# A two-layer diffusion trunk on one core: VectorE's head factors and scalings moved to other places, the convolution's tap split over two engines, a state-space product in two halves, and a shorter inverse root

## The chip, the cores and the metric

The kernel runs on one core of a Trainium2 chip. The metric is the device time of one execution in microseconds, as a median of several runs. A core has five engines that run their own instruction queues in order and meet at semaphores: TensorE (PE, its weight loads PEld), VectorE (DVE), ScalarE (ACT), GpSimd (POOL) and SyncE (SP), which here issues all DMAs.

## The reference, cut to what matters

Two layers. Each normalises and modulates the stream (512 latent and 256 context tokens, width 1024), projects it, runs four mixers on the projection, merges them by gates, and ends with a SwiGLU network. The change touches the inverse roots of all norms and these parts of three mixers:

```python
def rms_norm(x, g, eps=1e-6):
    y = xf * lax.rsqrt(jnp.mean(xf * xf, axis=-1, keepdims=True) + eps)
    return (y * g.astype(jnp.float32)).astype(x.dtype)

def sgu_branch(z, lp):                      # spatial gating
    u, v = jnp.split(jax.nn.gelu(z), 2, axis=-1)
    v = layer_norm(v, lp['sgu_ln_g'], lp['sgu_ln_b'])
    ...

def prep(p):                                # state-space duality
    z, xbc, dt_raw = split_cols(p, (BR_W, SSD_CONV_CH, 2 * SSD_HEADS))
    xbc = jax.nn.silu(conv_centred(xbc, lp['ssd_conv_w'], lp['ssd_conv_b']))   # three taps along the tokens
    ...
    return (y_diag + y_off).reshape(b, L, H, P), final      # ssd_scan: within a block, and from the state before it

def mla_qkv(p, lp):                         # latent attention, 6 heads
    q = (rms_norm(cq, lp['mla_q_a_norm']) @ lp['mla_w_uq']).reshape(bsz, L, MLA_HEADS, MLA_QK)
    kv = (rms_norm(ckv, lp['mla_kv_a_norm']) @ lp['mla_w_ukv']).reshape(bsz, L, MLA_HEADS, MLA_NOPE + MLA_V)
    k_nope, v = jnp.split(kv, [MLA_NOPE], axis=-1)
    k = jnp.concatenate([k_nope, jnp.broadcast_to(k_rope[:, :, None, :], ...)], axis=-1)
    return rms_norm(q, lp['mla_q_norm']), rms_norm(k, lp['mla_k_norm']), v

def rope_2d(t, cos, sin):                   # latent tokens only
    nope, rot = t[..., :MLA_NOPE], t[..., MLA_NOPE:]
    x1, x2 = jnp.split(rot, 2, axis=-1)
    return jnp.concatenate([nope, x1 * c - x2 * s, x1 * s + x2 * c], axis=-1)

def softmax_attend(q, k, v):
    pr = jax.nn.softmax(s, axis=-1).astype(v.dtype)
    return jnp.einsum('bhqk,bkhd->bqhd', pr, v)
```

## The kernel before, in words

All large products are made of three: weights and streams are split into a high and a low part (`whi`, `wlo`; `h`), and `mm3` adds low times high, high times high and high times low into one bank of PSUM. `proj` does this for one tile of 128 columns, 512 latent tokens and then 256 context tokens, in a bank named `acc`, of which there are two; smaller work takes one of four banks `b`, and the diagonal state space two more. A callback then takes the result out of the bank; the next product that wants the bank waits for the last read of it.

A layer's mixing (`mix`) is a set of generators that one loop advances in turn: the projections, latent attention's first half (`mla`: queries, then keys and values, two token tiles at a time in `mla_pair`), the diagonal state space (`five`), attention itself (`attend`, one unit for two heads and 256 queries in `attend_unit`, six to nine units a layer), spatial gating (`sgu`), the projections with the convolution (`conv`), and the dual state space (`ssd`). The order in which the instructions stand on each engine is made when the program is built, by a list scheduler with a time model of its own, from priorities that follow the code and `at(...)`. On the chip each engine then keeps that order.

The places that the change touches:
- `rsqrt`: a bit trick on the vector engine and three Newton steps of three operations, with `-x/2` made once: 11 instructions. It stands in 44 places, on tiles of 1 to 12 columns: 7 in `norm_mod`, 10 in `ssd`, 5 in `sgu`, and two for each of the 11 pairs of `mla_pair` (six in layer 0, five in layer 1).
- `mla_pair`, second half: `rr`, an inverse root for each token and head, goes over q or k together with the gain `gn` (`qn`, `kn`: the 96 gains, the same for all heads, on all partitions), by one `s.stt` for each head and tile: 12 a pair. The rotary key is multiplied by its gains into `kg`. GpSimd rotates with cosines and sines from the constant tile `k`. Six transposes bring a tile to [96, head, token]; ACT takes three of the heads out of PSUM, DVE the other three.
- `mla_pair`, first half: `v` goes out of PSUM with the factor `r`, by DVE: `s.ts(vt[:, b, hs, :], pv[:, :, 64:P], r[:, b:b + 1])`.
- `attend_unit`: ACT makes the exponentials with their sums, DVE adds the two sums and takes the reciprocal, and DVE multiplies each tile of probabilities (128 x 768, or 128 x 256 for context) by it, in place: four a unit. Their transposes come one unit later.
- `sgu`: DVE subtracts the mean and multiplies by the inverse root.
- `conv`: five operations on the result of a projection, in `cb`: DVE makes the middle tap with the bias out of `acc`, adds the left and the right tap, ACT writes the tanh back into `acc`, and DVE makes `(tanh + 1) a` from it.
- `ssd`: for every block of 128 tokens and each of three column tiles, a product with the identity brings `yoff` into the bank, and four products of 64 columns add the rest.

Of the kernel before, what the change touches and what calls it, by code (L numbers as in the profile page):

```python
# [19 lines left out]
P = 128  # L20
# [47 lines left out]
def pieces(segs):  # L68
    """starts of the 256-token pieces"""
    return [t for off, n, _ in segs for t in range(off, off + n, 256)]  # L70


class Cut:
    """one row of tokens in several tiles: [(first token, count, tile)]"""
# [11 lines left out]
class Net:  # L86
# [117 lines left out]
    def rsqrt(s, y, x):  # L204
        shape = list(x.shape)
        hx, t = s.ty(shape), s.ty(shape)
        s.ts(y.bitcast(I32), x.bitcast(I32), -0.5, float(0x5F3759DF), ALU.mult, ALU.add)
        s.ts(hx, x, -0.5)
        for _ in range(3):
            s.mul(t, y, y)  # L210
            s.mul(t, t, hx)
            s.stt(y, t, 1.5, y, ALU.add, ALU.mult)
# [54 lines left out]
    def tok_rsqrt(s, sq, nb, mul, eps):  # L267
        """per token (token-major) rsqrt(mul * sum over partitions and given tiles + eps)"""
# [50 lines left out]
    def params_rest(s, l, loaded):  # L319
# [19 lines left out]
        q["qn"], q["kn"] = bc("qn", t["mla_q_norm"][l], 96), bc("kn", t["mla_k_norm"][l], 96)  # L339
# [43 lines left out]
    def ada_chunk(s, a, i, raw=None):  # L383
        """columns 256 i .. of the modulation"""
# [26 lines left out]
    def cuts(s, segs, count):  # L411
        """rows of tokens in f tiles"""
# [35 lines left out]
    def norm_mod(s, xs, gs, sh, segs, hh, hl):  # L448
        """hi and lo of the modulated norm, a segment a step"""
# [23 lines left out]
    def weights(s, ap, c0, width, kt=KD, step=P, e=()):  # L473
        """yields (hi, lo, m) of the column tiles of ap[:, c0:c0+width]"""
# [35 lines left out]
    def gelu2(s, out, x):  # L510
        """2 gelu(x)"""
# [5 lines left out]
    def sgu_prep(s, l, q):  # L517
        """the spatial weights transposed; the bias takes in the layer norm's offset"""
# [17 lines left out]
    def sgu(s, q, wsT, uvd, segs, yd):  # L536
        for t0 in pieces(segs):
# [14 lines left out]
            s.rsqrt(r, x)  # L552
            for j in range(2):
                s.ts(vn[:, j, :], vn[:, j, :], mv[:, j, 0:1], r[:, j:j + 1], ALU.subtract, ALU.mult)
# [14 lines left out]
    def mla(s, l, q, xd, kd, segs, qk):  # L569
        """xd: cq^T and ckv^T in DRAM; kd: token-major [P, NB, 44] with the rotary key"""  # L570
# [27 lines left out]
    def mla_pair(s, part, q, kd, off, t0, b0, xd, nk, nw, wh, wl, qk):  # L598
        """two token tiles from t0: q or k, v, normalised, rotated, transposed"""
# [19 lines left out]
        for b in range(2):  # L619
# [3 lines left out]
            for j in range(2):  # L623
# [7 lines left out]
                if part == "kv":  # L631
                    s.ts(vt[:, b, hs, :], pv[:, :, 64:P], r[:, b:b + 1])
# [16 lines left out]
        gn = q["qn"] if part == "q" else q["kn"]  # L649
        e = s.nc.gpsimd  # L650
        for b in range(2):
            x, full = tiles[b]
            tb = t0 + b
            for h in range(6):
                s.stt(x[:, h, :w], x[:, h, :w], rr[:, b, h:h + 1], gn[:, :w], ALU.mult, ALU.mult)
            if part == "kv":
                kg = s.ty([P, 1, 32])
                s.mul(kg, kr[:, b:b + 1, :], gn[:, 64:].unsqueeze(1))
                s.mul(x[:, :, 64:96], kg.to_broadcast([P, 6, 32]), rs[:, b, :].unsqueeze(2).to_broadcast([P, 6, 32]))
            if off == CTX:  # L660
                cs, sn = (s.k[:, j + 16 * (b0 + b):j + 16 * (b0 + b) + 16].unsqueeze(1).unsqueeze(1).to_broadcast([P, 6, 2, 16])
                          for j in (K_COS, K_SIN))
# [10 lines left out]
            s.act(y[:, 0:3], ps[0][:96])  # L673
            s.vcopy(y[:, 3:6], ps[1][:96])
# [23 lines left out]
    def attend_unit(s, c, t0, nk, qs, ks, vs, yd):  # L698
        """two heads, 256 queries"""
        scale = 96.0 ** -0.5  # L700
        pr = []
        for h2 in range(2):
# [23 lines left out]
            for b in range(2):  # L726
                s.ts(p[b][:, :nk * P], p[b][:, :nk * P], ri[:, b:b + 1])
# [17 lines left out]
    def ssd(s, l, q, zd, xd, cd, kd, segs, yd):  # L745
        """zd: 2 silu(z)^T, xd: x^T and B^T, cd: C^T by group (zero rows of the other), all in DRAM; kd: token-major dt"""
# [828 lines left out]
```

## Time and profile before

| | |
|---|---|
| median of 3 runs | 2835.06 us (2834.6 to 2836.26) |
| the profiled execution: span from first to last instruction | 2833.9 us, 1.2 us under the median |
| TensorE matmul busy | 2639.4 us (93%) |
| VectorE busy | 1562.5 us (55%) |
| ScalarE, GpSimd busy | 870.4 us (31%), 1210.8 us (43%) |
| mean granted TensorE clock | 0.974 of full speed |

A busy time is the union of an engine's rows. A matmul's row covers its way through the array, so neighbouring rows overlap and a busy TensorE is not one at its peak. Behind a row stands the idle time of its engine just before it, and what ended it. The granted clock is 1 at 2.4 GHz and 0.5 at 1.2 GHz.

### The profile page before, as it was taken

How to read it: one execution, taken by the hardware profiler on the slowest of the kernel's cores; microseconds unless marked ns; L12 is line 12 of the kernel's file. 1: busy time of each engine (PE TensorE's matmuls, PEld its weight loads, DVE VectorE, ACT ScalarE, POOL GpSimd, SP SyncE). 2: the span in 40 equal slices, each digit the busy share in tenths (PEclk: the TensorE clock that was granted, in tenths of full speed). 3: DMA queues.
4: the chain of work that ended last, by engine and by line, in shares of the span. 5: the costliest groups of instructions: out<-in, count | busy, mean ns of one | idle time of the engine just before them, and what ended most of it. 6: DMA issues, size and time to landing. Idle time of an engine off the chain costs nothing. (4 is left out here: it accounts for less than half of the span.)

```text
span 2833.9 us, 40144 instructions
## 1 busy us (share of the span) xinstructions
PE 2639.4 (93%) x14950; PEld 2147.7 (76%) x14950; DVE 1562.5 (55%) x3402; ACT 870.4 (31%) x1693; POOL 1210.8 (43%) x901
## 2 busy tenths in 40 slices
PE   6998898999999987999999999899999989899999
PEld 4777676777888875888888877777666866678887
DVE  6678989758453769543221245677836546422111
ACT  4233332342232333222212234333343223322222
POOL 2254444314432836554333334442423537344543
PEclk9999899999999998999999999999999989999999
DMA  7655454454444645323322335556445536323332
GB/s 247 175 176 188 138 168 141 145 162 143 138 155 149 213 139 169 108 91 94 97 76 60 94 98 159 179 175 192 139 152 167 167 127 206 114 84 105 104 97 82
DMA packets 430106, 397.46 MB, mean 140 GB/s; under 512 B 52292, under 2 KB 379640, under 8 KB 429816
## 3 DMA queue, kind: packets, MB, share of 16 engines
q1 hardware_dynamic: 429912, 394.91, 45.4%
q8 instruction: 118, 1.93, 0.3%
q14 instruction: 76, 0.62, 0.1%
HBM read 305.79 MB, written 89.05 MB: 139 GB/s over the span
## 5 line engine op out<-in xcount | busy, mean ns | idle before, releaser
L174 POOL TENSOR_TENSOR wlo<-raw,whi 128x1024 fp32r<-128x1024 f32 (+2 forms) x314 | 632.3, 2015 | 1064.9 <-ACT whi L169 982.9
L193 PE MATMUL acc<-h,whi 128*128 128x512 f32 (+2 forms) x3424 | 1020.8, 368 | 30.6 <-DVE gs L186 22.6
L193 PE MATMUL acc<-h,wlo 128*128 128x512 f32 (+1 forms) x2024 | 745.8, 369 | 7.8 <-DVE wlo L174 5.1
L193 PEld LDWEIGHTS acc<-h,whi 128*128 128x128 f32 (+1 forms) x3424 | 612.0, 191 | 142.4 <-DVE gs L186 25.7
L169 ACT CAST whi<-raw 128x1024 fp32r<-128x1024 f32 (+2 forms) x390 | 324.9, 834 | 817.1 <-PE b L193 304.8
L193 PEld LDWEIGHTS acc<-h,wlo 128*128 128x128 f32 x2024 | 384.5, 190 | 76.4 <-DVE wlo L174 7.1
L193 PE MATMUL acc<-g,whi 128*128 128x512 f32 (+1 forms) x840 | 271.4, 396 | 20.4 <-DVE g L174 8.5
L193 PE MATMUL acc<-f,whi 128*128 128x512 f32 (+1 forms) x600 | 230.2, 393 | 6.3 <-POOL f L174 5.2
L193 PE MATMUL b<-g,whi 128*128 128x256 f32 (+1 forms) x840 | 215.7, 335 | 3.3 <-ACT whi L169 3.3
L193 PE MATMUL b<-h,wlo 128*128 128x256 f32 (+1 forms) x624 | 203.6, 326 | 2.1 <-POOL wlo L174 2.1
L193 PE MATMUL b<-h,whi 128*128 128x256 f32 (+1 forms) x624 | 203.4, 326 | 0.0
L193 PEld LDWEIGHTS acc<-g,whi 128*128 128x128 f32 x840 | 153.9, 193 | 56.4 <-DVE g L174 11.9
L193 PE MATMUL b<-f,whi 128*128 128x256 f32 (+1 forms) x600 | 186.7, 321 | 1.7 <-ACT whi L169 1.7
L193 PE MATMUL b<-g,g 128*64 128x128 f32 (+5 forms) x915 | 180.4, 357 | 8.0 <-ACT g L171 5.2
L193 PEld LDWEIGHTS b<-g,whi 128*128 128x128 f32 x840 | 148.8, 193 | 28.4 <-ACT whi L169 6.5
L193 PE MATMUL acc<-g,wlo 128*128 128x512 f32 (+1 forms) x372 | 148.2, 398 | 4.7 <-DVE wlo L174 4.5
L186 DVE SCALAR_TENSOR_TENSOR sc<-sc,acc 128x512 f32<-128x512 f32 (+1 forms) x45 | 30.6, 680 | 219.6 <-ACT sc L171 219.6
L193 PEld LDWEIGHTS b<-g,g 128*128 128x128 f32 (+2 forms) x915 | 121.1, 182 | 34.2 <-issue 13.5
L174 POOL TENSOR_TENSOR g<-sc,g 128x256 fp32r<-128x256 f32 (+2 forms) x81 | 88.2, 1090 | 126.7 <-ACT g L169 87.9
L193 PEld LDWEIGHTS acc<-f,whi 128*128 128x128 f32 x600 | 112.8, 189 | 31.5 <-POOL f L174 6.7
L174 POOL TENSOR_TENSOR f<-f,f 128x384 f32<-128x384 f32 (+2 forms) x84 | 102.8, 1229 | 78.7 <-DVE f L174 35.0
L174 POOL TENSOR_TENSOR g<-g,sc 128x512 f32<-128x512 f32 (+1 forms) x82 | 103.0, 1268 | 75.8 <-DVE g L186 37.9
(257 smaller groups left out, 4013.2 us busy)
## 6 DMA issues: line engine op xcount, KB each, us to landing
raw<-in_w_in_dram SPq DMA_DIRECT2D x50, 1024.0 KB
raw<-in_w_ffn_in_dram SPq DMA_DIRECT2D x88, 512.0 KB
raw<-in_w_ada_dram SPq DMA_DIRECT2D x41, 1024.0 KB
raw<-in_w_ffn_out_dram SPq DMA_DIRECT2D x36, 512.0 KB
gate<-gs SPq DMA_DIRECT2D x32, 384.0 KB
f<-s5w SPq DMA_DIRECT2D x48, 256.0 KB
raw<-in_w_branch_dram SPq DMA_DIRECT2D x32, 384.0 KB
gs<-gate SPq DMA_DIRECT2D x32, 384.0 KB
```

The costliest lines, as they stand in the source:

```text
L169: s.nc.scalar.copy(out=out, in_=x)
L174: (e or s.nc.vector).tensor_tensor(out=out, in0=a, in1=b, op=op)
L186: s.nc.vector.scalar_tensor_tensor(out=out, in0=a, scalar=sc, in1=b, op0=op0, op1=op1)
L193: s.nc.tensor.matmul(out=out, lhsT=l, rhs=r, start=start, stop=stop)
```

## The change

- `rsqrt` is one step of third order and one Newton step: nine instructions, each of which needs the one before it.
- The gains of q and k leave the vector engine's factors. One multiplication of a whole tile (six heads) by `rr` takes the place of six. The gains are applied where the transposed tile leaves PSUM: there a head's channels are the partitions, so the gain is one number a partition (`gain`, [96, 4]; its columns 1 and 3, used for latent tokens, hold 1 in the 32 rotary rows). For latent tokens the rotary gains are multiplied into tables of cosines and sines (`rotq`, `rotkv`) once a layer, with eight small products on DVE; `gain` takes four small DMAs a layer.
- The scaling of v, of the probabilities and of spatial gating's tokens goes from DVE to ACT (`sgu` has one small product on DVE more).
- The convolution's middle tap is ACT's; the tanh goes into a tile `sc` in SBUF instead of back into `acc`, and the last product reads that tile.
- The identity product of `ssd` is two of 64 columns.

All other lines of the diff take out comments.

```diff
     def rsqrt(s, y, x):
-        shape = list(x.shape)
-        hx, t = s.ty(shape), s.ty(shape)
+        t, u = s.ty(list(x.shape)), s.ty(list(x.shape))
         s.ts(y.bitcast(I32), x.bitcast(I32), -0.5, float(0x5F3759DF), ALU.mult, ALU.add)
-        s.ts(hx, x, -0.5)
-        for _ in range(3):
-            s.mul(t, y, y)
-            s.mul(t, t, hx)
-            s.stt(y, t, 1.5, y, ALU.add, ALU.mult)
+        s.mul(t, y, y)
+        s.mul(t, t, x)
+        s.ts(u, t, 0.375, -1.25, ALU.mult, ALU.add)
+        s.mul(u, u, t)
+        s.stt(y, u, 1.875, y, ALU.add, ALU.mult)
+        s.stt(t, y, -0.5, y, ALU.mult, ALU.mult)
+        s.mul(t, t, x)
+        s.stt(y, t, 1.5, y, ALU.add, ALU.mult)
...
+        gain = q["gain"] = s.keep("gain", [96, 4])
+        s.nc.vector.memset(gain, 1.0)
...
+                s.mul(gt[:, j], g, cs)
+            s.dma.dma_start(out=gain[:, 2 * i:2 * i + 1], in_=ap.rearrange("(d o) -> d o", o=1))
+            s.dma.dma_start(out=gain[:64, 2 * i + 1:2 * i + 2], in_=ap[:64].rearrange("(d o) -> d o", o=1))
...
             s.rsqrt(r, x)
+            s.stt(x, mv[:, :, 0], -1.0, r, ALU.mult, ALU.mult)
             for j in range(2):
-                s.ts(vn[:, j, :], vn[:, j, :], mv[:, j, 0:1], r[:, j:j + 1], ALU.subtract, ALU.mult)
+                s.act(vn[:, j, :], vn[:, j, :], AF.Identity, scale=r[:, j:j + 1], bias=x[:, j:j + 1])
...
-                    s.ts(vt[:, b, hs, :], pv[:, :, 64:P], r[:, b:b + 1])
+                    s.act(vt[:, b, hs, :], pv[:, :, 64:P], AF.Copy, scale=r[:, b:b + 1])
...
-            for h in range(6):
-                s.stt(x[:, h, :w], x[:, h, :w], rr[:, b, h:h + 1], gn[:, :w], ALU.mult, ALU.mult)
+            s.mul(x[:, :, :w], x[:, :, :w], rr[:, b, :].unsqueeze(2).to_broadcast([P, 6, w]))
             if part == "kv":
-                kg = s.ty([P, 1, 32])
-                s.mul(kg, kr[:, b:b + 1, :], gn[:, 64:].unsqueeze(1))
-                s.mul(x[:, :, 64:96], kg.to_broadcast([P, 6, 32]), rs[:, b, :].unsqueeze(2).to_broadcast([P, 6, 32]))
+                s.mul(x[:, :, 64:96], kr[:, b:b + 1, :].to_broadcast([P, 6, 32]), rs[:, b, :].unsqueeze(2).to_broadcast([P, 6, 32]))
...
-            s.act(y[:, 0:3], ps[0][:96])
-            s.vcopy(y[:, 3:6], ps[1][:96])
+            s.act(y[:, 0:3], ps[0][:96], AF.Copy, scale=gc)
+            s.ts(y[:, 3:6], ps[1][:96], gc)
...
             for b in range(2):
-                s.ts(p[b][:, :nk * P], p[b][:, :nk * P], ri[:, b:b + 1])
+                s.act(p[b][:, :nk * P], p[b][:, :nk * P], AF.Copy, scale=ri[:, b:b + 1])
...
                 if yoff is not None:
-                    s.mm(o, yoff[:, 2 * c:2 * c + 2, :].rearrange("p h e -> p (h e)"), s.ident, stop=False)
+                    for h2 in range(2):
+                        s.mm(o[64 * h2:64 * h2 + 64, :], yoff[:, 2 * c + h2, :], s.ident, stop=False)
...
                 a = y[:, off:off + n]
-                s.ts(a, ps, w(1), q["cb"][:, c:c + 1], ALU.mult, ALU.add)
+                s.act(a, ps, AF.Identity, scale=w(1), bias=q["cb"][:, c:c + 1])
                 s.stt(a[:, 1:n], ps[:, 0:n - 1], w(0), a[:, 1:n], ALU.mult, ALU.add)
                 s.stt(a[:, 0:n - 1], ps[:, 1:n], w(2), a[:, 0:n - 1], ALU.mult, ALU.add)
-                s.act(ps, a, AF.Tanh)
-                s.stt(a, ps, 1.0, a, ALU.add, ALU.mult)
+                z = s.sc()[:, :n]
+                s.act(z, a, AF.Tanh)
+                s.stt(a, z, 1.0, a, ALU.add, ALU.mult)
```

Three places show what the scheduler makes of it. The first is on VectorE, in layer 0, where the second query pair's tiles (`g_1795`, `g_1822` before; `g_1801`, `g_1828` after) get their factors; `ty` are the inverse roots. Before:

```order
L174 TENSOR_TENSOR ty_2087<-ty_2082 128x12
L174 TENSOR_TENSOR ty_2087<-ty_2087,ty_2086 128x12
L186 SCALAR_TENSOR_TENSOR ty_2082<-ty_2087,ty_2082 128x12
L174 TENSOR_TENSOR ty_2083<-ty_2082,ty_1777 128x12
L186 SCALAR_TENSOR_TENSOR g_1795<-g_1795,ty_2083,qn_317 128x96 x6
L186 SCALAR_TENSOR_TENSOR g_1822<-g_1822,ty_2083,qn_317 128x96 x6
L174 TENSOR_TENSOR sc_2191<-sc_2191 128x256
```

And after, on the same engine at the same place:

```order
L174 TENSOR_TENSOR ty_1956<-ty_1956,ty_1955 128x12
L174 TENSOR_TENSOR ty_2090<-ty_2090,ty_2085 128x12
L186 SCALAR_TENSOR_TENSOR ty_2086<-ty_2090,ty_2086 128x12
L174 TENSOR_TENSOR ty_2087<-ty_2086,ty_1785 128x12
L174 TENSOR_TENSOR g_1801<-g_1801,ty_2087 128x576
L174 TENSOR_TENSOR g_1828<-g_1828,ty_2087 128x576
L174 TENSOR_TENSOR sc_2183<-sc_2183 128x256
```

Twelve instructions became two, and the work around them stayed in place.

The second is on ScalarE, at the first head of layer 0's first attention unit: `g` are the tiles of probabilities, `ty` behind them the sums, `gs` the result of a projection. Before:

```order
L171 ACTIVATE g_4321,ty_4308<-b_4304,ty_4307 128x256
L171 ACTIVATE g_4321,ty_4312<-b_4313,ty_4307 128x512
L171 ACTIVATE g_4322,ty_4308<-b_4304,ty_4307 128x256
L171 ACTIVATE g_4322,ty_4312<-b_4316,ty_4307 128x512
L171 ACTIVATE acc_4405<-gs_4404 128x512
L169 CAST whi_4744<-raw_4742 128x1024
```

After, from the same exponentials on:

```order
L171 ACTIVATE g_4233,ty_4220<-b_4216,ty_4219 128x256
L171 ACTIVATE g_4233,ty_4224<-b_4225,ty_4219 128x512
L171 ACTIVATE g_4234,ty_4220<-b_4216,ty_4219 128x256
L171 ACTIVATE g_4234,ty_4224<-b_4228,ty_4219 128x512
L171 ACTIVATE g_4233<-g_4233,ty_4221 128x768
L171 ACTIVATE g_4234<-g_4234,ty_4221 128x768
L171 ACTIVATE gs_4055<-acc_4056 128x512
```

The two scalings stand right behind the exponentials, ahead of the eviction of a bank `acc`; `ty_4221` is DVE's reciprocal of the sums.

The third is on VectorE, where the convolution's first tile (`gs`) is made in layer 0. Before:

```order
L190 TENSOR_SCALAR gs_4404<-acc_4405,hc_311 128x512
L174 TENSOR_TENSOR ty_4308<-ty_4308,ty_4312 128x2
L186 SCALAR_TENSOR_TENSOR gs_4404<-acc_4405,hc_311,gs_4404 128x511
L725 RECIPROCAL ty_4309<-ty_4308 128x2
L708 TENSOR_REDUCE ty_4334<-b_4331 128x2
L186 SCALAR_TENSOR_TENSOR gs_4404<-acc_4405,hc_311,gs_4404 128x511
L190 TENSOR_SCALAR g_4321<-g_4321,ty_4309 128x768
L190 TENSOR_SCALAR g_4322<-g_4322,ty_4309 128x768
L714 TENSOR_REDUCE ty_4338<-b_4340 128x1
L714 TENSOR_REDUCE ty_4338<-b_4343 128x1
L186 SCALAR_TENSOR_TENSOR gs_4404<-acc_4405,gs_4404 128x512
```

After:

```order
L174 TENSOR_TENSOR ty_4247<-ty_4247,ty_4251 128x2
L735 RECIPROCAL ty_4248<-ty_4247 128x2
L174 TENSOR_TENSOR f_5086<-f_5086,f_5087 128x512
L186 SCALAR_TENSOR_TENSOR gs_4315<-acc_4316,hc_311,gs_4315 128x511 x2
L186 SCALAR_TENSOR_TENSOR gs_4315<-sc_4344,gs_4315 128x512
L174 TENSOR_TENSOR f_5261<-f_4882,f_4880 128x512
L174 TENSOR_TENSOR f_5263<-f_4882,f_4880 128x512
L186 SCALAR_TENSOR_TENSOR gs_4315<-acc_4347,hc_311,gs_4315 128x255 x2
```

Before, the bank `acc_4405` was read last by the eleventh of these rows, with the probabilities and two maxima between; now it is read last by the second of two neighbouring taps.

## Rows read from the trace of the kernel before

**Rows 1.** The page's busy time: us, share of the span, instructions.
```profile
PE 2639.4 (93%) x14950; PEld 2147.7 (76%) x14950; DVE 1562.5 (55%) x3402; ACT 870.4 (31%) x1693; POOL 1210.8 (43%) x901
```
**Rows 2.** Windows: us, busy PE, PEld, DVE, ACT, POOL, granted clock, DMA share, GB/s.
```profile
160.00:355.00 195.00, 162.48 (x1070) 140.27 (x1070) 171.41 (x451) 67.62 (x158) 97.64 (x94) 0.93 0.50 157
355.00:640.00 285.00, 261.43 (x1659) 203.09 (x1659) 217.70 (x471) 103.21 (x261) 100.83 (x90) 0.96 0.51 154
...
1768.00:1930.00 162.00, 148.81 (x920) 124.04 (x919) 116.81 (x337) 60.67 (x133) 72.58 (x75) 0.97 0.58 178
1930.00:2140.00 210.00, 198.31 (x1169) 146.19 (x1168) 137.47 (x297) 78.35 (x186) 61.62 (x48) 0.99 0.50 155
```
**Rows 3.** Timeline of PE and DVE at 249 us: start, length, what, idle before.
```profile
249.21 0.42 PE L197 MATMUL b<-k,g 128*96 128x128 f32 x1 [11.68 <-DVE g L186]
...
248.75 2.83 DVE L186 SCALAR_TENSOR_TENSOR g<-g,ty,qn 128x96 f32<-128x96 f32 x12
```
**Rows 4.** Timeline of DVE and PE around a convolution tile at 463 us.
```profile
462.87 0.53 DVE L190 TENSOR_SCALAR gs<-acc,hc 128x256 f32<-128x256 f32 x1
463.32 3.16 DVE L190 TENSOR_SCALAR g<-g,ty 128x256 f32<-128x256 f32 x2
...
474.21 0.40 DVE L186 SCALAR_TENSOR_TENSOR gs<-acc,gs 128x256 f32<-128x256 f32 x1
...
474.67 0.80 PE L193 MATMUL acc<-h,whi 128*128 128x256 f32 x2 [5.06 <-DVE gs L186]
```
**Rows 5.** DVE's groups by shape: busy us, mean ns, idle before.
```profile
L190 DVE TENSOR_SCALAR g<-g,ty 128x768 f32<-128x768 f32 x48 | 31.2, 690 | 0.3
...
L174 DVE TENSOR_TENSOR g<-g,sc 128x768 f32<-128x768 f32 x20 | 30.1, 1507 | 15.6 <-ACT g L171 15.6
...
L186 DVE SCALAR_TENSOR_TENSOR g<-g,ty,qn 128x96 f32<-128x96 f32 x60 | 23.5, 463 | 0.1
L174 DVE TENSOR_TENSOR f<-f,f 128x384 f32<-128x384 f32 x30 | 23.2, 772 | 0.1
...
L186 DVE SCALAR_TENSOR_TENSOR g<-g,ty,kn 128x64 f32<-128x64 f32 x72 | 21.7, 365 | 0.0
...
L174 DVE TENSOR_TENSOR ty<-ty 128x2 f32<-128x2 f32 x68 | 19.6, 289 | 1.4
...
L190 DVE TENSOR_SCALAR g<-b,ty 128x192 f32<-128x192 f32 x24 | 9.5, 413 | 6.7 <-ACT st L171 6.6
...
L186 DVE SCALAR_TENSOR_TENSOR g<-sc,g 128x256 f32<-128x256 f32 x15 | 8.3, 571 | 0.3
...
L190 DVE TENSOR_SCALAR gs<-acc,hc 128x512 f32<-128x512 f32 x10 | 8.0, 804 | 1.4 <-PE acc L193 1.4
...
L190 DVE TENSOR_SCALAR g<-g,ty 128x256 f32<-128x256 f32 x12 | 7.0, 621 | 0.1
...
L190 DVE TENSOR_SCALAR gs<-acc,hc 128x256 f32<-128x256 f32 x9 | 4.8, 531 | 0.9 <-PE acc L193 0.9
...
L186 DVE SCALAR_TENSOR_TENSOR gs<-acc,gs 128x256 f32<-128x256 f32 x9 | 3.7, 413 | 0.1
```
**Rows 6.** ACT's groups by shape.
```profile
L171 ACT ACTIVATE g<-b,ty 128x256 f32<-128x256 f32 x60 | 28.3, 473 | 70.2 <-DVE ty L190 64.3 <-DVE ty L174 3.3 <-DVE ty L186 1.7
...
L171 ACT ACTIVATE g<-st,prm 128x768 fp32r<-128x768 f32 x4 | 3.8, 938 | 9.3 <-DMA st<-in_mla_w_ukv_dram 9.1 <-ACT gs L171 0.2
```
**Rows 7.** Timeline of PE at an output block of layer 1's `ssd`.
```profile
2211.67 0.49 PE L193 MATMUL b<-k,sc 128*128 128x128 f32 x2
2212.08 0.66 PE L193 MATMUL b<-g,g 128*64 128x128 f32 x8
2212.67 0.49 PE L193 MATMUL b<-k,sc 128*128 128x128 f32 x2
```
**Rows 8.** Timeline of DVE in the last inverse root of layer 1's `ssd`.
```profile
2309.11 0.16 DVE L174 TENSOR_TENSOR ty<-ty 128x1 f32<-128x1 f32 x1
2309.30 0.16 DVE L174 TENSOR_TENSOR ty<-ty,ty 128x1 f32<-128x1 f32 x1
```

More of the change, by code (lines that the diff above doesn't have):

```diff
@@ L338, in params_rest @@
         q["dtb"] = bc("dtb", t["ssd_dt_bias"][l].rearrange("a b -> (a b)"), 12)
-        q["qn"], q["kn"] = bc("qn", t["mla_q_norm"][l], 96), bc("kn", t["mla_k_norm"][l], 96)
+        q["rot"] = {}
+        gain = q["gain"] = s.keep("gain", [96, 4])
+        s.nc.vector.memset(gain, 1.0)
+        for i, (part, ap) in enumerate((("q", t["mla_q_norm"][l]), ("kv", t["mla_k_norm"][l]))):
+            g = bc("gn" + part, ap[64:96], 32).rearrange("p (o a d) -> p o a d", o=1, a=2).to_broadcast([P, 4, 2, 16])
+            gt = q["rot"][part] = s.keep("rot" + part, [P, 2, 4, 2, 16])
+            for j, c in enumerate((K_COS, K_SIN)):
+                cs = s.k[:, c:c + 64].rearrange("p (b o d) -> p b o d", b=4, o=1).to_broadcast([P, 4, 2, 16])
+                s.mul(gt[:, j], g, cs)
+            s.dma.dma_start(out=gain[:, 2 * i:2 * i + 1], in_=ap.rearrange("(d o) -> d o", o=1))
+            s.dma.dma_start(out=gain[:64, 2 * i + 1:2 * i + 2], in_=ap[:64].rearrange("(d o) -> d o", o=1))
         bs = s.keep("bs", [P, 3, P])
@@ L648, in mla_pair @@
         s.mul(rr, rs, r.unsqueeze(2).to_broadcast([P, 2, 6]))
-        gn = q["qn"] if part == "q" else q["kn"]
+        gt, gc = q["rot"][part], q["gain"][:, 2 * (part == "kv") + (off == CTX):][:, :1]
         e = s.nc.gpsimd
@@ L653, in mla_pair @@
             tb = t0 + b
-            for h in range(6):
-                s.stt(x[:, h, :w], x[:, h, :w], rr[:, b, h:h + 1], gn[:, :w], ALU.mult, ALU.mult)
+            s.mul(x[:, :, :w], x[:, :, :w], rr[:, b, :].unsqueeze(2).to_broadcast([P, 6, w]))
             if part == "kv":
-                kg = s.ty([P, 1, 32])
-                s.mul(kg, kr[:, b:b + 1, :], gn[:, 64:].unsqueeze(1))
-                s.mul(x[:, :, 64:96], kg.to_broadcast([P, 6, 32]), rs[:, b, :].unsqueeze(2).to_broadcast([P, 6, 32]))
+                s.mul(x[:, :, 64:96], kr[:, b:b + 1, :].to_broadcast([P, 6, 32]), rs[:, b, :].unsqueeze(2).to_broadcast([P, 6, 32]))
             if off == CTX:
-                cs, sn = (s.k[:, j + 16 * (b0 + b):j + 16 * (b0 + b) + 16].unsqueeze(1).unsqueeze(1).to_broadcast([P, 6, 2, 16])
-                          for j in (K_COS, K_SIN))
+                cs, sn = (gt[:, i, b0 + b].unsqueeze(1).to_broadcast([P, 6, 2, 16]) for i in range(2))
                 xr = x[:, :, 64:96].rearrange("p h (a d) -> p h a d", a=2)
```

## The prediction, made before the changed kernel ran

> **What bounds the kernel now.** First the table of busy time: TensorE is busy for 93% of the span, VectorE for 55%, ScalarE for 31% [rows 1]. So the limit over the whole is TensorE, and a change that takes nothing from it can win only where TensorE waits: at most 2833.9 - 2639.4 = 194.5 us, and what the slow clock costs after waits. Then the windows, to see where that is. The change sits in four stretches, latent attention's first half and attention itself, of layer 0 (160 to 355, 355 to 640 us) and of layer 1 (1768 to 1930, 1930 to 2140), 852 us in all. There VectorE is busy for 171.4 of 195, 217.7 of 285, 116.8 of 162 and 137.5 of 210 us (88, 76, 72 and 65%), and TensorE idles for 32.5, 23.6, 13.2 and 11.7 us, 81 us together; the granted clock is 0.93, 0.96, 0.97 and 0.99 [rows 2]. In the first stretch VectorE is all but full: it paces, and TensorE stands between.
>
> Two timelines show how. At 249 us TensorE has waited 11.7 us for one transpose of q's heads; what ended the wait is the row of twelve factors on VectorE, 2.83 us long, at the end of VectorE's queue of other work [rows 3]. At 474.7 us it has waited 5.1 us for a bank `acc`: the convolution's middle tap is made at 462.9, two scalings of probabilities then take 3.2 us, and the last read of the bank comes at 474.2 [rows 4], 11.7 us after the first. There are only two such banks.
>
> **The change part by part.** I sum the work that leaves VectorE in the four stretches, and then choose how much of it reaches the end.
>
> Removed: the head factors, 60 and 72 instructions, 23.5 + 21.7 = 45.2 us; the scalings of probabilities, 31.2 + 7.0 = 38.2; those of v, 9.5; the middle taps, 8.0 + 4.8 = 12.8 [rows 5]. Spatial gating's ten scalings are bought with ten small products, and I set both to nothing. `rsqrt` has two instructions fewer; 27 of its 44 calls stand in these stretches (two for each of 11 pairs, five in `sgu`), and at 0.289 us for such an instruction, waits for GpSimd included [rows 5], that is 27 x 2 x 0.289 = 15.6. Together 121 us.
>
> Added: one product of 128 x 576 for each of ten q tiles and one of 128 x 384 (six heads of 64) for each of twelve k tiles. The trace has such a product at 128 x 384, 0.772 us, and at 128 x 768, 1.507 us [rows 5], about 2 ns a column either way: 10 x 1.15 + 12 x 0.77 = 20.7. (Lower bound: the middle taps, which read PSUM, take 0.804 us at 512 columns and 0.531 at 256 [rows 5], 1.07 ns a column; at that, with 0.1 us to start, 576 and 384 columns cost 0.7 and 0.5, 13 us in all.) The convolution's last product now reads two SBUF tiles instead of PSUM and SBUF: 0.571 against 0.413 us at 256 columns [rows 5], so 0 to 0.3 us for each of 19; I take 3 us. Three heads now leave PSUM with a factor a partition instead of as a copy, 22 times. The row for such an operation from PSUM is v's, 0.413 us for 192 columns [rows 5]; I take 0.1 us more each, 2 us (bounds 0 and 22 x 0.4 = 9). The eight table products stand at the start, under the wait for weights. Added: 26 us. Net about 95 us of VectorE's 643 in these stretches, 15%.
>
> By stretch: first halves 45.2 + 9.5 + 12.7 (22 calls) - 20.7 - 2 = 44.7, split by pairs 6 to 5: 24 and 20. Attention 38.2 + 12.8 + 2.9 - 3 = 50.9, split by units 9 to 6: 31 and 20.
>
> How much of it is time? Nothing, if TensorE is the pace; all of it up to TensorE's idle time, if VectorE is: 24 + 23.6 + 13.2 + 11.7 = 72.5. In the first stretch, with VectorE at 88% and the longest wait ending on the very instruction that shrinks, I take 0.6 of 24: 14. In the others, where VectorE is full for a part of the stretch only, 0.35: 11, 7 and 7. Sum **39 us**, a little over half of the upper bound. This includes the earlier release of `acc`: its last read is now the second tap, not a product that waits for the tanh.
>
> The identity product is on TensorE's own path. A whole one takes 0.41 us from its start to that of the next (2211.67 to 2212.08), and eight rows of 64-column products 0.59 (2212.08 to 2212.67), 0.074 a row [rows 7]. In halves it is four such rows, 0.30. There are 30: 30 x 0.11 = **3 us** (bounds 0, if only the order changes, and 6). The rows show that 64-column products cost less a row than the identity product between them; the Trainium skill (TensorEngine Tiling (Array Packing), Key Properties) says that a change of tiling mode drains the engine, which fits the dearer row at the change of shape. The same page (Instruction Overhead) charges every matmul some 60 cycles, and by that alone doubling the instructions would make this term a loss of 60 more rows x 0.025 = 1.5 us, as an estimate from that page.
>
> The inverse roots on the critical path: each instruction starts 0.19 us after the one it needs [rows 8]. Ten steps in a row (the factor `hx` stood beside them) become nine, so 0.2 us for each of the seven calls in `norm_mod` and the last one in each `ssd`: 9 x 0.2, about **2 us**, and 1 to be careful, since not each is waited for.
>
> What ScalarE takes on: scalings of 768 columns with a factor a partition at 0.938 us [rows 6] for 0.690 on VectorE [rows 5], 48 x 0.94 + 12 x 0.5 = 51 us, and some 30 us of v, taps and gating. It is busy for 309.9 of the 852 us [rows 2], so there is room, 542 us of it; but its queue is in order, and scalings that wait for VectorE's reciprocal hold up the eviction behind them. I take **5 us** against the change for this (bounds 0 and the first rival). The slower clock is a gain that I leave out of the sum: in the first stretch 0.93 means that TensorE ran at 1.2 GHz for 14% of 195 us, which is at most 13.6 us at the other level, and a few us in the rest.
>
> Small DMAs: eight a layer where there were two with gains; those of layer 1 follow a VectorE memset but stand among loads for work far ahead. Nothing.
>
> Sum: 2833.9 - 39 - 3 - 1 + 5 = 2796 in the span; the median of the runs lies 1.2 us over this execution's span, so **2797 us**, 1.3% less.
>
> **The rivals.**
> (a) *ScalarE's round trip makes it slower.* The scalings stand directly behind the exponentials in ScalarE's new order, ahead of an eviction of `acc`. For each of 30 heads of units it must wait until VectorE, in its own order, has added the sums and taken the reciprocal. How long such a hand-over takes is seen where ScalarE already waits for VectorE's maximum: 64.3 us in front of the first exponentials [rows 6], 2.1 us over their 30 heads. At 2.1 to 4.3 us (twice that) for each of 30, ScalarE stands for 63 to 129 us; the change loses if TensorE gets more than 38 of it. With half of 129 it would be 2797 + 64 = 2861, and I set this case at **2850**. For it: the order, and only two banks. Against it: ScalarE's 542 free us, and TensorE's work from other branches in between. The Trainium skill (ScalarE: Activation LUTs, Rules for kernel authors) tells to keep multiplications on VectorE. Its rule would put the scalings' 48 x 0.25 = 12 us on the path of the units by the two rows above, and this is the case in which it holds.
> (b) *Nothing moves.* TensorE is the pace already, the waits that go are replaced by waits for the next late thing (GpSimd's parts, state-space loads), and only the identity product and the roots count: 2835 - 4 = **2831**. For it: 93% busy. Against: waits of 5 to 12 us that end on just these rows.
> (c) *VectorE was the pace throughout.* Then all 72.5 us come back, and about 16 of the clock's: 2797 - 33 - 16 - 5 = **2743**. Against: in layer 1 VectorE is busy for 65 to 72% only.
>
> **How the numbers follow.** Forecast case, 2755 to 2828: 0.70. (a) 0.14, (b) 0.09, (c) 0.07. A measurement of this kernel can tell about 0.2% (6 us) from no change. Faster: the forecast, (c) and a third of (b), 0.80; same: the rest of (b), 0.06; slower: (a), 0.14. The range of 8 in 10 is 2752 to 2842: it leaves out most of (a) and (c).
>
> **What would show it.** VectorE's busy time should fall by 90 to 130 us to 1430 to 1470, ScalarE's rise by about 80. The groups with `qn` and `kn` are gone, with new ones of 128 x 576 and 128 x 384 at 0.6 to 1.2 us. In the list of TensorE's waits, those that end on the tap tile `gs` and on the twelve factors should shrink from 5 and 12 us to under 3. The identity's four rows should take about 0.3 us. I would be wrong if ScalarE's waits for the reciprocal add up to over 60 us and TensorE's waits for banks follow them; or if TensorE's idle time in the four stretches stays at 80 us under other names.

## The result and the profile after

The changed kernel takes 2791.8 us (median of 4 runs, 2787.4 to 2795.3) where the kernel before, on the same chip, takes 2834.8 (4 runs, 2829.4 to 2836.3): ratio 0.9856, 95% interval 0.9841 to 0.9872, 41 us or 1.4% faster (the two medians themselves lie 43 us apart). The forecast was 2797 us.

The table of busy time of the changed kernel (answers to [rows 1]):

```profile
span 2787.8 us, 40075 instructions
PE 2626.8 (94%) x15010; PEld 2140.9 (77%) x15010; DVE 1475.8 (53%) x3094; ACT 941.8 (34%) x1806; POOL 1210.0 (43%) x901
```

VectorE lost 86.7 us and ScalarE gained 71.4. The span is 46.1 us shorter: TensorE idles for 161.0 us instead of 194.5, and is busy for 12.6 us less. To see where, the windows of the kernel before, cut at marks that both kernels have: the attention's first product for q in layer 0, the first load of the hidden layer's weights, the same product in layer 1, and the last load of the merging there (columns as in rows 2).

```profile
0.00:164.80 164.80, 137.29 (x826) 106.53 (x827) 105.58 (x357) 58.47 (x106) 50.33 (x46) 0.96 0.69 214
164.80:1077.00 912.20, 835.59 (x5214) 689.61 (x5212) 654.64 (x1425) 297.07 (x650) 399.86 (x324) 0.97 0.50 157
1077.00:1768.90 691.90, 663.48 (x3822) 568.26 (x3823) 287.05 (x502) 181.29 (x314) 308.26 (x216) 0.98 0.34 102
1768.90:2385.90 617.00, 575.13 (x3215) 442.81 (x3213) 395.85 (x950) 208.58 (x447) 255.11 (x204) 0.97 0.54 166
2385.90:2833.90 448.00, 427.94 (x1880) 340.49 (x1879) 119.34 (x172) 124.94 (x176) 197.20 (x114) 0.99 0.35 102
```

And of the changed kernel, cut at the same marks:

```profile
0.00:162.90 162.90, 137.84 (x827) 106.29 (x827) 108.06 (x358) 58.55 (x106) 50.45 (x46) 0.95 0.68 217
162.90:1049.10 886.20, 831.83 (x5250) 687.02 (x5248) 596.07 (x1259) 336.53 (x714) 397.89 (x324) 0.97 0.52 161
1049.10:1740.50 691.40, 665.11 (x3822) 570.00 (x3823) 285.20 (x494) 181.71 (x314) 308.86 (x216) 0.97 0.34 102
1740.50:2339.70 599.20, 564.80 (x3238) 437.09 (x3237) 366.33 (x817) 239.98 (x496) 255.53 (x204) 0.98 0.55 171
2339.70:2787.80 448.10, 427.18 (x1880) 340.53 (x1879) 120.11 (x171) 125.03 (x176) 197.25 (x114) 0.99 0.35 101
```

Nearly all of it lies in the two stretches of mixing: 26.0 us in layer 0 and 17.8 in layer 1, 2.3 everywhere else. In layer 0 it is mostly idle time: 912.2 - 835.6 = 76.6 us became 54.4. In layer 1 the idle time fell only from 41.9 to 34.4, and TensorE's busy time fell by 10.3: the granted clock rose from 0.97 to 0.98, and the identity's rows are in there. Such a split of one execution is rough. By the same marks layer 1's mixing takes 609 us with the inverse root alone and 606 with the bank's release alone, instead of 617, and neither of these two kernels gains time; so some 10 us of a stretch can come and go without the change. A mark inside a stretch would mislead: in layer 1 the last score product moved ahead by 60 us (2130.8 to 2070.9), but the merging began only 30 us earlier (2284.5 to 2254.9), because other branches' products that had run between the scores now run after them: between the two marks stand 987 rows of TensorE instead of 836.

TensorE's waits before, in the list of who waited for whom (total us, times, longest):

```profile
PE acc L193 <- DVE gs L186: 22.6, 9, 5.1
...
PE b L197 <- DVE g L186: 13.0, 3, 11.7
...
PE b L193 <- DVE sc L443: 11.0, 7, 3.5
```

And after:

```profile
PE b L193 <- DVE sc L190: 12.3, 4, 5.3
...
PE b L197 <- DVE g L174: 11.0, 2, 9.9
...
PE acc L193 <- DVE gs L186: 6.9, 8, 1.8
...
PE acc L193 <- ACT gs L171: 2.2, 3, 1.3
...
PE b L193 <- DVE sc L456: 2.1, 1, 2.1
```

The wait for a bank `acc` behind the tap tile was 22.6 us with a longest of 5.1 [rows 4] and is 6.9 with a longest of 1.8. The waits for VectorE's copies out of a bank `b` (`sc`, L443 before, L456 after) fell from 11.0 us to 2.1. But the long wait for the twelve factors [rows 3], 11.7 us, is still there at 9.9: only its last row has another name (`g`, a product, where it was a row of factors). VectorE around it, in time order, then the transposes that waited:

```profile
237.55 3.51 DVE L456 COPY ty<-ty 64x64 f32<-64x64 f32 x2
...
241.07 1.49 DVE L174 TENSOR_TENSOR f<-ty,f 128x512 f32<-128x512 f32 x1
242.49 1.01 DVE L186 SCALAR_TENSOR_TENSOR ty<-ty,ty 128x12 f32<-128x12 f32 x1
243.54 0.17 DVE L174 TENSOR_TENSOR ty<-ty,ty 128x12 f32<-128x12 f32 x1
243.75 1.43 DVE L174 TENSOR_TENSOR g<-g,ty 128x576 f32<-128x576 f32 x2
...
244.65 1.49 PE L197 MATMUL b<-k,g 128*96 128x128 f32 x6 [9.92 <-DVE g L174]
```

The factors themselves take 1.43 us instead of 2.83. What is late is the steps of the inverse root, and between them stand tables of the state-space branch, two copies of 64 x 64 for 3.5 us among them.

The groups that are new, VectorE's first, then ScalarE's (busy us, mean ns of one, idle before) (answers to [rows 5, 6]):

```profile
L190 DVE TENSOR_SCALAR g<-b,gain 96x384 f32<-96x384 f32 x22 | 13.0, 603 | 9.5 <-PE b L197 8.3 <-POOL g L174 1.2
L174 DVE TENSOR_TENSOR g<-g,ty 128x384 f32<-128x384 f32 x12 | 11.8, 1023 | 0.0
L174 DVE TENSOR_TENSOR g<-g,ty 128x576 f32<-128x576 f32 x10 | 7.1, 754 | 0.1
```

```profile
L171 ACT ACTIVATE g<-g,ty 128x768 f32<-128x768 f32 x48 | 42.5, 938 | 16.3 <-DVE ty L735 16.3
L171 ACT ACTIVATE g<-b,ty 128x256 f32<-128x256 f32 x60 | 28.3, 473 | 46.9 <-DVE ty L190 40.0 <-PE b L193 4.8 <-DVE ty L186 2.1
L171 ACT ACTIVATE g<-b,ty 128x192 f32<-128x192 f32 x24 | 9.8, 435 | 9.5 <-DVE ty L186 9.5
L171 ACT ACTIVATE gs<-acc,hc 128x512 f32<-128x512 f32 x10 | 7.8, 781 | 8.0 <-PE acc L193 7.9
L171 ACT ACTIVATE g<-g,ty 128x256 f32<-128x256 f32 x12 | 5.5, 508 | 4.1 <-DVE ty L735 4.1
```

ScalarE stands for 16.3 + 4.1 = 20.4 us in front of its scalings until VectorE's reciprocal is there, 0.7 us for each of 30 heads of units, and its older wait for the maximum fell from 64.3 [rows 6] to 40.0.

The identity product in TensorE's timeline (answers to [rows 7]):

```profile
2145.62 0.44 PE L193 MATMUL b<-k,sc 128*64 128x128 f32 x4
2145.89 0.39 PE L193 MATMUL b<-g,g 128*64 128x128 f32 x4
```

Four identity rows start 0.27 us ahead of what follows, 0.068 a row. This is the first identity product of its block; the other two take 0.22 us in most blocks. Over all 30, from the first row to the start of what follows, 12.6 us became 7.2: 5.4 us, of which 0.9 are three products before that stood at a granted clock of 0.5 and took 0.72 us each.

### The profile page after: what moved, and what is told of

Its sections match the earlier page's. It is cut to its first block, busy times and chain, and to the rows that moved or that the text cites. A ratio compares the mean times of both kernels' runs of the same rounds, so it can differ in the third digit from the quotient of the medians.

```text
span 2787.8 us, 40075 instructions
## 1 busy us (share of the span) xinstructions
PE 2626.8 (94%) x15010; PEld 2140.9 (77%) x15010; DVE 1475.8 (53%) x3094; ACT 941.8 (34%) x1806; POOL 1210.0 (43%) x901
```

## The experiments

Each ratio is to the kernel before, run beside it on the same chip; its medians there were 2834.9, 2833.5 and 2833.0 us on three chips. Microseconds gained are worked out from the ratios. What is read from a trace is one execution.

The prediction's theory is **VectorE's queue**: a microsecond of VectorE's time inside the mixing is worth some 0.4 us, since TensorE waits for whatever stands at the queue's end. Against it stand **the bank** (the convolution's gain comes from freeing `acc` earlier), **the round trip** (the scalings on ScalarE cost a hand-over, or gain by sparing one), and **the order** (every edit gives the scheduler another order, and the sizes of the edits explain little).

The first six put one part, or a piece of one, into the kernel before, as it stands in the change's diff.

**The inverse root alone.** Edit: the function `rsqrt` of the change.

> Only the nine-instruction inverse root is put into the kernel before. Queue theory (VectorE's queue paces the mixing, and about 0.4 of the work that leaves it comes back as time): 88 instructions at 0.2 to 0.29 us leave VectorE, 18 to 25 us, of which 16 stand in the mixing stretches, so 6 us faster and 1 to 2 more at the norms: 4 to 10 us faster. Bank theory (the early release of the projection's bank is the cause): 1 to 2 us faster, from the norms alone. Order theory (any change rearranges the whole schedule, and the parts do not add up): anything from 10 us faster to 10 us slower.

2838.8 us, ratio 1.0017 (1.0005 to 1.0029). VectorE's busy time fell by 22.0 us (1562.5 to 1540.5), and the kernel did not become faster; the wait for `acc` behind `gs` is 25.9 us there, its longest 8.6. The queue theory expected 4 to 10 us less. So 22 us of VectorE can be worth nothing.

**The head factors alone.** Edit: the lines of `mla_pair` and of the parameters, the first of them:

```
-            for h in range(6):
-                s.stt(x[:, h, :w], x[:, h, :w], rr[:, b, h:h + 1], gn[:, :w], ALU.mult, ALU.mult)
+            s.mul(x[:, :, :w], x[:, :, :w], rr[:, b, :].unsqueeze(2).to_broadcast([P, 6, w]))
```

> Only the head factors change: one product over six heads, the gains at the eviction and in the rotary tables. Queue theory: VectorE loses 45 us of factors and gets 21 to 23 back, so 22 to 24 us less, and the wait of TensorE at 249 us falls from 11.7 us to under 9; 10 us faster (5 to 15). Bank theory: 0 to 3 us faster. Order theory: -10 to +10.

2820.2 us, ratio 0.9942 (0.9925 to 0.9960), 16 us, for 17.7 us of VectorE's busy time. The wait for the factors fell to 8.9 us. But by the marks the gain isn't where the work left: layer 0's mixing, where VectorE is busy for 18.6 us less, is 1.6 us shorter (910.6), layer 1's, with 1.2 us less of VectorE, 18.5 (598.5). The granted clock was 0.96 and 0.99 there, where before it was 0.97 and 0.97. So one execution doesn't show that this gain is the queue's.

**The scalings alone.** Edit: probabilities, v and the gating's normalisation; the line for the probabilities:

```
-                s.ts(p[b][:, :nk * P], p[b][:, :nk * P], ri[:, b:b + 1])
+                s.act(p[b][:, :nk * P], p[b][:, :nk * P], AF.Copy, scale=ri[:, b:b + 1])
```

> Only the scalings of probabilities, of v and of spatial gating go to ScalarE. Queue theory: VectorE loses 48 us (38 of probabilities, 9.5 of v) and the kernel is 17 us faster (10 to 25). Round-trip theory (ScalarE stands in its queue for VectorE's reciprocal and holds up evictions): 0 to 20 us slower, with over 60 us of ScalarE's idle time ended by the reciprocal. Bank theory: 0 to 3 us faster, or slower.

2810.6 us, ratio 0.9920 (0.9904 to 0.9935), 23 us, for 67.7 us of VectorE's, of which the moved scalings of probabilities and v make 48 [rows 5]; rows that the edit doesn't touch became shorter in this order, by some 18 us of added durations. Both mixings are shorter, by 12 and 15 us. ScalarE waited 16.8 us for the reciprocal, where the round-trip theory wanted over 60: a cost of the round trip that outweighs the gain is excluded. The Trainium skill (ScalarE: Activation LUTs, Rules for kernel authors) tells to keep a multiplication on VectorE; a scaling of 768 columns does take longer on ScalarE, 0.938 us for 0.690, and this kernel is faster with it there all the same; ScalarE is busy for 33% of the span.

**The convolution alone.** Edit: the middle tap to ScalarE, the tanh into an SBUF tile.

```
-                s.ts(a, ps, w(1), q["cb"][:, c:c + 1], ALU.mult, ALU.add)
+                s.act(a, ps, AF.Identity, scale=w(1), bias=q["cb"][:, c:c + 1])
...
-                s.act(ps, a, AF.Tanh)
-                s.stt(a, ps, 1.0, a, ALU.add, ALU.mult)
+                z = s.sc()[:, :n]
+                s.act(z, a, AF.Tanh)
+                s.stt(a, z, 1.0, a, ALU.add, ALU.mult)
```

> Only the convolution changes: the middle tap on ScalarE, the tanh into SBUF, so that the last read of the bank is the second tap. Queue theory: VectorE loses 13 us and gets 0 to 6 back; together with the earlier release 6 us faster (3 to 12), and TensorE's waits on the tap tile fall from 22.6 us to under 10. Bank theory: 20 to 35 us faster, most of the whole change. Order theory: -10 to +10.

2817.8 us, ratio 0.9942 (0.9925 to 0.9958), 16 us, for 12.4 us of VectorE's. That is more than VectorE's time should give, and less than the bank theory's 20 to 35; the waits on the tap tile fell to 16.2 us only, not under 10. The bank is still a suspect:

**The bank's release alone.** Edit: of the lines above only the last five, with the middle tap left on VectorE.

> The kernel before with one piece of the convolution's edit alone: the tanh goes to an SBUF tile instead of back into the bank, and the last product reads that tile. VectorE's work does not shrink (it grows by 0 to 3 us), but the bank is free two instructions earlier. If the bank's release is what the convolution's edit gained (ratio 0.9942 for 12.8 us of VectorE's time), most of its 16 us come here: 2820 to 2828. If it was VectorE's 12.8 us of taps, nothing comes: 2832 to 2838.

2832.1 us, ratio 0.9997 (0.9986 to 1.0009). The release gives nothing by itself. What gains is the tap on ScalarE, alone or together with the release; why it is worth more than its 12.8 us isn't shown. One thing the trace does show: TensorE's waits for the copies out of `b` are 1.0 us with the convolution's edit, 9.9 with the release alone, 11.0 before. They are small in the other two runs that gain 16 us or more (factors 2.7, scalings 3.3) and larger in those that gain 5 us or nothing (identity 7.4, root 6.2). These copies are VectorE's too, so a shorter queue would show there; what the tap has to do with them is not tested.

**The identity alone.** Edit: the halves in `ssd`.

```
-                    s.mm(o, yoff[:, 2 * c:2 * c + 2, :].rearrange("p h e -> p (h e)"), s.ident, stop=False)
+                    for h2 in range(2):
+                        s.mm(o[64 * h2:64 * h2 + 64, :], yoff[:, 2 * c + h2, :], s.ident, stop=False)
```

> The kernel before with the identity product in two halves alone. By the prediction's step 30 x 0.11 us come back: 2832 us, 0.1% less (bounds 2829 and 2835), and the four identity rows take 0.30 us instead of 0.41. If a change of order alone moves this kernel by some us, as the inverse root alone suggests (0.17% slower with less work), the time can lie anywhere within 0.3% of before while the rows still get shorter.

2827.5 us, ratio 0.9982 (0.9970 to 0.9993), 5 us (2 to 8.5). The rows agree: all 30 products together take 7.2 us here too, 5.4 less than before, 4.5 without the three at the slow clock.

The five parts taken alone add up to -16 - 23 - 16 - 5 + 5 = -55 us, the whole gives -41. That fits parts that take time from the same waits, but the difference of 14 us has itself a width of some 10, from the widths of the six ratios.

The next undo something in the changed kernel. A ratio to the changed kernel is the quotient of the two ratios to before, its width from both widths, squared and added.

**The old inverse root in the changed kernel.** Edit: `rsqrt` as before.

> The changed kernel with the 11-instruction inverse root put back. If the shorter root really costs time (its nine steps in a row, where the eleventh and a tenth stood beside them), the kernel becomes faster by 3 to 5 us here too: 2787. If the shorter root is worth what the prediction gave it (1 us of path, 15.6 us of VectorE's queue, of which 0.35 to 0.6 counts), it becomes slower by 4 to 9 us: 2796 to 2801. If the sign of the single test came from the order of instructions, the two tests disagree in sign and both stay within 0.3%.

2798.7 us, 0.9880 of before (0.9866 to 0.9894), 1.0024 of the changed kernel (1.000 to 1.0045). Here the short root helps, if anything; alone it did harm. VectorE's busy time differs by 2.9 us only (1478.7), where alone it differed by 22: it isn't a fixed sum, since untouched rows change with the order.

**The probabilities' scalings back on VectorE.** Edit: the second line of the scalings' diff, undone.

> The changed kernel with the scalings of the probabilities back on VectorE (38 us there, some 50 us less on ScalarE). By VectorE's queue it is slower by 13 to 20 us, 2805 to 2812, and about as slow as with the useless work of the same length. If the units now wait for ScalarE's scalings (the round trip), it is not slower: 2785 to 2792.

2806.2 us, 0.9909 of before (0.9895 to 0.9923), 1.0054 of the changed kernel (1.003 to 1.0075): 15 us slower (9 to 21) for 36.0 us of VectorE's busy time, 0.42 us for each. A round trip that costs would have shown as no loss.

**Useless work instead of the scalings, first form.** Edit: behind each scaling on ScalarE, products on a scratch tile.

```
                 s.act(p[b][:, :nk * P], p[b][:, :nk * P], AF.Copy, scale=ri[:, b:b + 1])
+                for w in ((256, 256, 256) if nk == NB else (256,)):
+                    s.ts(s.junk[:, :w], s.junk[:, :w], 1.0)
```

> The changed kernel with extra work on VectorE that nothing reads: behind each reciprocal, three products of 128 x 256 on a scratch tile of its own where the scaling of 768 columns stood, one where that of 256 stood; the scalings stay on ScalarE. VectorE's busy time grows by 40 to 50 us. If it is the time in VectorE's queue that counts, the gain of the scalings is lost: 0.35 to 0.5 of it comes back, 2806 to 2815 us. If the scalings' gain came from ScalarE's place for them (no hand-over back to VectorE, another order), the time stays within 0.2% of 2792. If VectorE were the pace throughout, all of it: 2835.

2789.7 us, 0.9849 of before (0.9834 to 0.9864): no loss. It doesn't test what it was made for. The tile's page says where the work went:

```profile
L190 DVE TENSOR_SCALAR junk<-junk x156: 261/294/2270, 1.2 to 99.2; 128x256 f32<-128x256 f32 x156
```

Nothing held the products, so the scheduler put all 156 into the first 99 us. There they made the first product for q 12 us later (162.9 to 175.2), and the end 3 us earlier: by the marks, layer 0's mixing gave back little (3.4 us), and layer 1's was 10 us shorter, with no useless work in it but another order of the same instructions. So this run too shows some 10 us of a stretch that no removed work explains.

**Useless work in its place.** Edit: the product reads the reciprocal, so that it can't run ahead.

```
+                for _ in range(nk // 2):
+                    s.ts(s.junk, s.k[:, :256], ri[:, b:b + 1])
```

> The changed kernel with work on VectorE that nothing reads, this time bound to its place: products of 128 x 256 of a constant with the reciprocal, three for each scaling of 768 columns and one for each of 256, so that they cannot run ahead as in the first form. VectorE's busy time grows by 40 to 50 us within attention. If VectorE's queue is what the scalings cost, 14 to 23 us of the gain are lost: 2806 to 2815, as with the scalings themselves put back (2806). If it was the hand-over from VectorE to TensorE's transposes that the scalings cost, the time stays at 2786 to 2798.

2813.5 us, 0.9932 of before (0.9914 to 0.9950), 1.0077 of the changed kernel (1.005 to 1.010): 21.5 us slower (15 to 28). Its busy table and its useless rows:

```profile
PE 2629.0 (94%) x15010; PEld 2138.3 (76%) x15010; DVE 1535.5 (55%) x3250; ACT 942.2 (34%) x1806; POOL 1215.5 (43%) x901
```

```profile
L190 DVE TENSOR_SCALAR junk<-k,ty x156: 321/353/2502, 366.8 to 2109.5; 128x256 f32<-128x256 f32 x156
```

VectorE is busy for 59.7 us more, so 0.36 us are lost for each, though nobody reads the work. This is the strongest evidence for the queue, and for its size in attention: 0.36 and 0.42 from two experiments, with their widths 0.25 to 0.6, where the prediction took 0.35. The marks of the profiled executions give less. Of 20.9 us here, 5.8 are lost before the attention's first product for q, where TensorE and VectorE have the same rows in the same order as in the changed kernel and only the granted clock is lower (0.90 for 0.95); the two mixings lose 16.0 for 63.5 us of VectorE's, 0.25. With the probabilities back they lose 11.1 for 40.4, 0.27. In TensorE's list the waits for the copies out of `b` (`sc`, L457) are back, five with 11.0 us together as before the change (with the probabilities back they had stayed at 1.5), and the longest of these, at 571.8 us, ends like this:

```profile
564.82 3.51 DVE L457 COPY ty<-ty 64x64 f32<-64x64 f32 x4
568.34 2.78 DVE L174 TENSOR_TENSOR f<-ty,f 128x512 f32<-128x512 f32 x1
571.04 0.68 DVE L457 COPY sc<-b 128x512 f32<-128x512 f32 x1
...
571.77 1.53 PE L193 MATMUL b<-sc,g 128*64 128x256 f32 x6 [4.79 <-DVE sc L457]
```

A copy of 0.68 us was late behind 6 us of tables.

**A change of order with hardly any work.** Edit: one product of 128 x 2 for each pair, in the kernel before.

```
         s.mul(r2, r, r)
+        s.ts(s.junk, r2, 1.0)
```

> The kernel before with one product of 128 x 2 more for each pair of the attention's first half, 22 in all and some 4 us of VectorE; nothing reads them. It moves many instructions to other places on all engines. By the size of the work it is 0 to 2 us slower than before, 2834 to 2837. If the order alone is worth some us in this kernel, as the inverse root's two opposite signs suggest, the time lies anywhere from 2824 to 2846 and by its share outside 0.1%.

2834.0 us, ratio 1.0006 (0.9990 to 1.0021). In the traces' order (names without their numbers) some 1000 of TensorE's 14950 rows stand elsewhere, about as many as with the convolution or the scalings alone, and the time is the same within 0.2%. So another order need not move the kernel. One other order doesn't bound what order can do, though: the root's two signs (0.17% and 0.24%) may be of that kind, and single stretches moved by 10 us in runs that gained nothing.

**The copies to ScalarE.** Edit: in the changed kernel, all 48 copies of 64 x 64, of which two stood in the 9.9-us wait.

```
-            s.vcopy(bbs[e][0:64], bbr[64 * e:64 * e + 64])
-            s.vcopy(bbs[e][64:P], bbi[64 * e:64 * e + 64])
+            s.act(bbs[e][0:64], bbr[64 * e:64 * e + 64])
+            s.act(bbs[e][64:P], bbi[64 * e:64 * e + 64])
```

> The changed kernel with 48 copies of 64 x 64 in the state-space tables moved from VectorE to ScalarE, where they take less than 0.3 us each; on VectorE they take 32.8 us, and two of them, 3.5 us, stand in VectorE's queue inside the longest wait that is left, 9.9 us at 244.65. By VectorE's queue 0.35 to 0.6 of 32.8 us comes back, 11 to 20: 2772 to 2781, and the wait at 244.65 shrinks by about 3 us. If the copies lie under other work, or ScalarE's queue is the next bound, it stays within 0.3% of 2792.

2788.1 us, 0.9835 of before (0.9814 to 0.9857), 0.998 of the changed kernel (0.995 to 1.0005): the best median of all kernels here, but not told apart from the changed kernel: anything from 13 us faster to 2 slower. The queue at a flat rate expected 11 to 20 us. VectorE's busy time fell by 24.7 us; the copies take 11.6 us on ScalarE for 32.8 on VectorE; the longest wait for `g` is 5.2 us instead of 9.9, and the identity's first product in layer 0 comes 12 us earlier (685.2 to 673.4). Then it is given back in the profiled execution, which is the slowest of its four. TensorE's waits, and VectorE just before the end of the longest of them, 5.7 us until 380.37:

```profile
PE acc L193 <- DVE gs L186: 19.2, 9, 5.7
...
PE b L197 <- DVE g L174: 7.7, 3, 5.2
```

```profile
375.75 2.37 DVE L174 TENSOR_TENSOR ty<-f,f 128x64 f32<-128x64 f32 x1
378.05 0.54 DVE L174 TENSOR_TENSOR f<-f,f 128x384 f32<-128x384 f32 x1
378.52 0.83 DVE L186 SCALAR_TENSOR_TENSOR sx<-f,b 64x384 f32<-64x384 f32 x1
379.19 0.21 DVE L174 TENSOR_TENSOR ty<-ty,ty 128x64 f32<-128x64 f32 x1
379.31 1.01 DVE L186 SCALAR_TENSOR_TENSOR gs<-gs,acc 128x256 f32<-128x256 f32 x2
```

Tables stand in VectorE's queue in front of the last read of an `acc` bank, and these waits add up to 12 us more than in the changed kernel (19.2 for 6.9). In layer 0's mixing TensorE idles for 54.2 us, in the changed kernel for 54.4.

## Why the prediction was right

- **What bounds it** held. The gain came where the prediction looked, in the two mixings, and nearly nothing outside. TensorE's idle time was the room: 33.5 of 194.5 us came back. That VectorE's queue is what TensorE waits for is shown for the scalings of the probabilities, by taking them out (with v's and the gating's), putting them back and putting useless work in their place. For the factors and the convolution's tap it is argued only.
- **The fraction of VectorE's saving that counts**, 39 of 95 us (0.41), held as a mean: without the identity's 5 us, 36 us for the 86.7 that VectorE lost, 0.42. In attention the 0.35 was tested twice and measured 0.42 and 0.36 by the medians, 0.27 and 0.25 by the marks of one execution. As a rate it is no constant: 0.9 for the factors alone, over 1 for the convolution, and nothing for the root. So that the sum came out 5 us from the measured time is in part luck: 0.6 and 0.35 were choices between nothing and all, and the parts alone lie far from them on both sides. By layers the forecast had 25 us and 14 for the queue, without the identity; the marks show 26.0 and 17.8, of which the identity's 18 and 12 products are 2.4 and 3.0 by their rows.
- **Where layer 1's part comes from** was mis-stated: the forecast took it from idle time, which fell by 7.5 us; 10.3 came as TensorE's busy time, and only 3.0 of these are the identity's. The granted clock, which the sum left out as a gain, was 0.970 before and 0.977 after there, which is worth about half of the 10.3 us. How much of this belongs to the change is open: TensorE's busy time in this stretch is 4 to 6 us lower with the root or the release alone too.
- **VectorE's busy time** was to be 1430 to 1470 and is 1475.8. The removed groups are gone as counted, but the eight table products, put at nothing, take 4.5 + 3.3 = 7.8 us (four of them, 1.7 us, don't stand at the start but at 222 and 306 us, in layer 0's mixing); the twelve products of 128 x 384 take 1.02 us instead of 0.77 (those of 576 take 0.75 instead of 1.15: both together 18.9 against 20.7); and groups of unchanged number became longer, `f<-f,f` of 64 x 190 from 18.4 us to 25.8 and `ty<-ty,ty` of 128 x 12 from 15.5 to 20.8. Two smaller readings were off: the 0.1 us to start in the lower bound stands in no row (its own two rows, carried back to no columns, leave 0.26), and the small DMAs are six a layer, not eight.
- **The wait on the twelve factors** was to shrink from 12 us to under 3. This failed: 9.9 us. The step took the instruction that ended the wait for its cause. The queue ahead of it made it, tables and the root's steps in turns, and the copies' experiment, which took 3.5 us of that queue away, brought the longest such wait to 5.2. That is one execution with another order besides.
- **The wait on the tap tile** shrank as said (5.1 to 1.8 us), but the reason given beside it, the bank's earlier release, gave nothing by itself: 17.8 us of such waits are left with the release alone, of 22.6, and no time is gained. (In its reading of the tile at 463 us, the 11.7 us reach to the end of the last read; from start to start it is 11.3.)
- **The identity**: 3 us forecast, 4.5 by the rows at the full clock and 5 by the runs, inside its bounds. The Trainium skill (TensorEngine Tiling (Array Packing), Instruction Overhead) would have made the doubled instructions a loss of 1.5 us as estimated; rows that start 0.068 us apart and the run alone contradict that.
- **The inverse root**, 1 us on the path and part of 15.6 in the queue: open. It was 0.17% slower alone and 0.24% faster in the changed kernel, and a change of order alone isn't excluded from giving either.
- **ScalarE's cost**, 5 us, can't be read as one number; the signs are of less. Its busy time rose by 71 us (forecast about 80). The rival (a) needed 63 to 129 us of waits for the reciprocal, there were 20.4, and TensorE's waits for ScalarE's `g` add up to 1.8 us. Rival (b) falls with the result and the idle time, (c) with the useless work, which cost a quarter to a third of its length, and with the copies: 24.7 us less of VectorE gave no idle time back in the profiled execution.

## What to carry to other kernels

An in-order engine that feeds the bounding one has no single price: useless work in the middle of attention cost 0.25 to 0.36 us a microsecond, the same kind of work at the start showed no cost at the end, and taking 25 us of copies away moved the longest wait and gained nothing that the runs can tell. So sum what leaves the queue by stretch, take a fraction between nothing and all, and expect parts that gain 55 us one by one to gain 41 together. To find what a wait is made of, read the queue ahead of the row that ends it, not that row; and cut stretches at marks outside the mixing, since work of other branches crosses those inside. Even then one execution of each kernel doesn't tell apart stretches that differ by less than some 10 us.

## What the runs showed of the hardware

One and the same VectorE instruction, a product of 128 x 256 from and to SBUF with one tensor input, took from 0.32 to 2.50 us (median 0.35) in one execution. The 64 x 64 copies show the same: 0.68 us in the mean on VectorE, 0.24 on ScalarE. In the rows at 237.55 two of them take 3.5 us while GpSimd works on products of 128 x 512 and 128 x 1024 from 237.45 to 241.0. The trace of the changed kernel, read copy by copy, has 24 that take 0.63 to 2.29 us, each of them under rows of GpSimd for at least 94% of its length, and 24 that take 0.17 to 0.19 us, all but four of them with GpSimd idle for most of theirs. The useless products split in the same way: the seven longer than 1 us lie under GpSimd's rows for 94% of their time, the 141 of up to 0.4 us for 2%. So the length of a row on VectorE's queue goes with what GpSimd does beside it, which would be one way in which a new order changes VectorE's busy time. The Trainium skill (SBUF — State Buffer, Who interferes with whom) says that VectorE and GpSimd share a pair of ports, and that copies and products with a scalar can take it in a two-port mode; the rows fit that closely, but no experiment here took GpSimd's work away, so that it is the cause isn't shown.
